# A two-layer hybrid trunk on one core: the recurrence's inverse as two factors with a squared matrix, and values products of causal attention for two blocks of queries at a time

## Chip, cores and metric

The kernel runs on one core of a Trainium2 chip. A core has TensorE (PE: matmuls and transposes, with its weight loads in a row of their own, PEld), VectorE (DVE), ScalarE (ACT), GpSimd (POOL) and SyncE (SP, which here only issues the loads and stores, "DMA"). The metric is the time of one execution of the whole program on the device in microseconds (us); the result is a median of several runs.

## The reference

The input is x, 512 positions of width 1024, with 256 memory tokens. Each of two layers projects x onto about 10,000 columns, feeds four branches of width 512 from them, multiplies each by a gate, projects it back, adds them up with sigmoid gates, projects once more and normalizes with the residual. The change touches two branches and the gate of one.

```python
for l in range(DEPTH):
    h = x @ w_in[l]
    ...
    y_rwkv = _rwkv7_branch(rw_p, rw_g, ...)     # recurrence, 8 heads of 64
    y_mla = _mla_branch(q_lat, kv_lat, ...)     # causal attention, 8 heads
    y_conv = ...; y_mem = ...
    proj = einsum('bsnc,ncd->bsnd', stack(branches), w_o_branch[l])
    merged = sum(sigmoid(merge + b_gate[l]) * proj, axis=2)
    x = layer_norm(ALPHA * x + merged @ w_out[l])

# recurrence, per head, state 64x64, one step per position t
sa = einsum('bhvk,bhk->bhv', state, a_t)
state = state * w_t + sa[..., None] * b_t + v_t[..., None] * k_t
y_t = einsum('bhvk,bhk->bhv', state, r_t)       # then group norm, bonus, * silu(gate)

# causal attention, 128 queries at a time
s = einsum('bqhd,bkhd->bhqk', q_blk, k) * scale     # masked to key <= query
o = einsum('bhqk,bkhd->bqhd', softmax(s), v)
```

## The kernel before

**Wide matmuls.** Activations lie channel by channel: 128 channels on the partitions, 512 positions in the free dimension. The projections are matmuls of a 128x128 weight block with a 128x512 activation. For precision weights and activations are split into a high and a low part (w48h, w48l; xh, xl), and each product is made of three matmuls, of type fp32r. There are thousands of these, and they depend on little else, so they serve as filler under everything that has a chain. In the trace their targets are called ps_m (merge gates), po (output of a branch), ps_rg (gate of the recurrence's branch) and so on; mt, tm and merged are the gated sums on VectorE; w214 is the 214th weight block.

**Order of the work.** The program is written out by `Plan` (lines 59 to 190), which keeps an approximate clock for each engine while it is built. There is a stream of wide items and a list of small tasks (Python generators). At each point the plan takes a task whose operands are due and otherwise the next item. A task that yields "small" runs small matmuls; it is held up to 3000 ns (GATHER) so that several tasks' small matmuls stand together. `shape` charges a switch of the array's cut. The costs used are in `MM` (lines 264 to 284), `Engine.call` and `dma`. The order of each engine is then fixed: on the chip an engine takes its instructions in exactly this order and waits where an operand is not there. So in the trace nearly all matmuls have line 282 (`MM`), transposes 287, operations of VectorE, ScalarE and GpSimd 231 and loads 294, and they are told apart by names.

**The recurrence** (`rwkv_unit`) handles 64 positions at once in closed form. A unit is one pair of heads with four such chunks, half of the sequence: 4 pairs times 2 halves times 2 layers are 16 units. A unit needs the inverse of a 64x64 matrix with unit diagonal, made from a strictly triangular M, for two heads and four chunks: eight 64x64 problems. All small matmuls use a quarter of the array (64x64 cut), four at a time ("quads"), in fp32; each leaves two rows in the trace.

- The four 16x16 diagonal blocks are inverted by substitution on GpSimd (lines 792 to 831): M's blocks go through memory (scr) to W, then 14 steps, and the inverse and its transpose come back through memory as zc and tc (16 columns per block). Z and T are the same, spread by the mask bm to block-diagonal 64x64 tiles.
- Two levels then double the block, from 16 to 32 and to 64 (lines 887 to 952), each with two matmul stages and an evacuation between. x0: M times half the columns of T (width 32), with NQ times vt (nv, an operand of a later step) in the same stage; ScalarE copies to X, VectorE copies nv to RA. dt, dz: Z times X and X times Z (width 32); VectorE copies them with the masks lvm into T and Z (`copy_predicated`). x1: M times T, copied to X. dy: X times Z, copied by mask into Z. X is zeroed once per layer and only partly overwritten.
- va is then Z times RA, followed by the gb/hh/y0 products, the four-step chain of states (w0 to w3) and yb, the output. VectorE takes statistics of yb (gs, gm), GpSimd a power (gr), VectorE scales yb, TensorE transposes it (ty), and yr is the branch's output.

**Causal attention** (`pair`, `mla_block`, lines 1400 to 1478): per layer four pairs of heads; per pair four blocks of 128 queries for each of two heads. A block computes scores (ms), softmax (mP), its transposes (mt) and their copy on ScalarE (mPT, at most four buffers of 512 columns). When both heads' block i is there, their products with the values follow as one "small" group: 2(i+1) matmuls of a 128x64 cut into mo. So there are groups of 2, 4, 6 and 8 matmuls (twice as many rows), four per pair.

**Gates.** `gate_items` multiplies a branch's output by silu of its projection. rg (number 0, the recurrence's) may start when the whole recurrence is done (`"rwkv" in L`), so it comes at the layer's end, ahead of the last merge.

Of the kernel before, what the change touches and what calls it, by code (L numbers as in the profile page):

```python
# [46 lines left out]
for _n, _c in _PARTS:  # L47
# [5 lines left out]
    ("ident", 128), ("bones2", 2), ("reset", 256), ("rn", 8), ("mstr", 64),  # L53
    ("minc", 64), ("bm", 4), ("id2", 64),
# [207 lines left out]
def trunk_kernel(ctx: ExitStack, tc: tile.TileContext, A, out, dbg=None):  # L262
# [4 lines left out]
    def MM(o, lhsT, rhs, start, stop, four=False):  # L267
# [5 lines left out]
        if m <= 64 and n < 16:  # L273
            c = 20.0
        elif rhs.dtype != F32 or n < 16:
            c = max(0.4167 * n + 13.0, 109.0) * (2 if rhs.dtype == F32 else 1)
        elif m <= 64:
            c = (0.42 if four else 0.83) * n + 1.0
        else:
            c = 1.667 * n + 5.0  # L280
# [57 lines left out]
    ident, bones2, reset = cc("ident"), cc("bones2"), cc("reset")  # L338
    lvm = cp.tile([128, 3, 64], U8, tag="lvm", name="lvm")
# [17 lines left out]
    def constants():  # L357
        DMA(cst, A["cst"])
        t = u("lvm32", 192, I32)
        DMA(t, A["lvm"])  # L360
# [5 lines left out]
        def run():  # L366
            V.tensor_copy(lvm, t.rearrange("p (a b) -> p a b", a=3))
# [227 lines left out]
    def layer_items(l):  # L595
# [62 lines left out]
        def begin_rwkv(get):  # L658
# [7 lines left out]
            L["X"] = L["rp"].tile([128, 4, 64], F32, tag="X", name="X" + t_)  # L666
            G.memset(L["X"], 0.0)
# [46 lines left out]
        def rwkv_unit(j, hf, r, k, v):  # L714
# [72 lines left out]
            for b in range(1, 4):  # L787
                V.scalar_tensor_tensor(out=Mc, in0=M[:, :, 16 * b:16 * b + 16], scalar=bm[:, b:b + 1], in1=Mc, op0=ALU.mult, op1=ALU.add)
            d1, d2 = scr[un % 2]
# [4 lines left out]
            def substitution():  # L794
# [27 lines left out]
                zc, tc_ = rk2("zc", "zc" + t, [4, 16], 2), rk2("tc", "tc" + t, [4, 16], 2)  # L822
# [5 lines left out]
                zt.extend((zc, tc_))  # L828
# [57 lines left out]

            yield lambda: L["subs"] > un
            zc, tc_ = zt
            plan.due(zc, tc_)
            yield  # L890
            Z, T, X = rk2("Z", "Z" + t, [4, 64]), rk2("T", "T" + t, [4, 64]), L["X"]
            for dst, src in ((T, tc_), (Z[:, 0:2], chunks(zc)[:, 0]), (Z[:, 2:4], chunks(zc)[:, 1])):
# [5 lines left out]
            def second(x, i):  # L898

                return x.rearrange("p e (d i k) -> p e d i k", d=2, i=2)[:, :, :, i, :]  # L900

            def pairs(x, i):
                return x.rearrange("p e w -> p (e w)").rearrange("p (e q i k) -> p e q i k", e=2, q=4, i=2)[:, :, :, i, :]

            def four(x):
# [1074 lines left out]
```

## Time and profile before

| | |
|---|---|
| median of 3 runs | 1552.19 us (1551.77 to 1552.38) |
| the profiled execution, own time | 1550.24 us |
| its span in the trace | 1548.5 us |
| instructions | 30167 |
| bytes moved by DMA | 153.21 MB, mean 99 GB/s |
| mean granted TensorE clock | 0.997 |

How to read it: a line of the timeline has the start in us from the span's start, the duration, engine, line, operation, out<-in, rows by columns of the array used, and the shape. "x16" are sixteen rows in sequence, and "[2.12 <-DVE yb L231]" is idle time ahead of the instruction with what ended it. Matmuls overlap in the pipeline: a duration is longer than the distance to the next start, and it is the starts that count. A line of the groups has the busy time in all and the mean in ns, then the idle time ahead of them. A line of the windows has the stretch, its length, the busy time of each engine with the number of instructions, the granted clock, the share of the DMA engines and GB/s.

### The profile page before, as it was taken

The page shows a single profiled execution, that of the slowest core. Times are in us where ns is not written, and L with a number is a line of the kernel's source. Part 1 is how long each engine was busy: PE and PEld are TensorE (multiplying, and loading weights), DVE is VectorE, ACT ScalarE, POOL GpSimd, SP SyncE. Part 2 cuts the span into 40 slices and gives each one's busy share as a digit, 9 for nine tenths or more (in the row PEclk, how much of TensorE's full clock was granted, in tenths as well). Part 3 has the DMA queues.
Part 4 walks back from the last instruction along what each step waited for, and adds up shares of the span by engine and source line. Part 5 has one row for each costly group of instructions (what it writes and reads, how often), then busy time and mean ns, then how long its engine had stood idle before and what let it go on. Part 6 is the DMA issues. An engine that isn't in the chain of part 4 may idle for free.

```text
span 1548.5 us, 30167 instructions
## 1 busy us (share of the span) xinstructions
PE 1519.8 (98%) x11912; PEld 1248.3 (81%) x11912; DVE 1111.7 (72%) x2488; ACT 642.3 (41%) x1387; POOL 237.5 (15%) x588
## 2 busy tenths in 40 slices
PE   8999999999999999999999999999999999999997
PEld 8878788877777777888998877788777777777886
DVE  6789888888567765545655888888876777645747
ACT  5546654433244332343364464534334343323332
POOL 0000000433214330000000000002533323300002
PEclk9999999999999999999999999999999999999999
DMA  6452422322222232423343234223222222225231
GB/s 211 129 158 65 116 82 82 90 88 61 86 85 63 72 92 83 149 96 126 123 140 119 83 102 118 75 95 96 65 85 75 75 78 75 75 96 177 95 113 65
DMA packets 81358, 153.21 MB, mean 99 GB/s; under 512 B 33216, under 2 KB 39360, under 8 KB 81216
## 3 DMA queue, kind: packets, MB, share of 16 engines
q1 hardware_dynamic: 81216, 151.28, 31.2%
q8 instruction: 93, 1.52, 0.4%
q14 instruction: 49, 0.40, 0.1%
HBM read 133.95 MB, written 5.77 MB: 90 GB/s over the span
## 4 chain that ended last, share of the span: by engine, by line
PE 86%; DVE 5%; DMA 3%; ACT 2%; POOL 1%; issue 1%; SPq 0%; ACTq 0%; DVEq 0%; POOLq 0%
PE ps_m L282 22%; PE po L282 11%; PE ps_mg L282 3%; PE ps_k L282 3%; PE ps_r L282 3%; PE ps_rg L282 3%; PE ps_v L282 3%; PE ps_xg L282 3%; PE ps_cg L282 3%; PE ps_xq L282 3%; PE ms L282 2%; PE ps_glu L282 2%; PE pz L282 2%; PE pl L282 2%; PE ps_val L282 2%; PE mo L282 1%
## 5 line engine op out<-in xcount | busy, mean ns | idle before, releaser
L231 DVE SCALAR_TENSOR_TENSOR cacc<-hpad,prm,cacc 128x512 f32<-128x512 f32 x240 | 180.2, 753 | 3.5
L231 ACT ACTIVATE tm<-ps_m,prm 128x512 f32<-128x512 f32 x64 | 44.1, 689 | 170.4 <-PE ps_m L282 166.2
L231 POOL TENSOR_TENSOR ZT<-ZT,tmpW 32x14 f32<-32x14 f32 (+6 forms) x224 | 85.7, 383 | 17.6
L231 POOL TENSOR_TENSOR tmpW<-ZT,W 32x14 f32<-32x14 f32 (+6 forms) x224 | 84.1, 375 | 16.1
L231 DVE SCALAR_TENSOR_TENSOR mt<-tm,po 128x512 f32<-128x512 f32 x48 | 33.0, 687 | 74.4 <-PE po L282 69.3
L231 POOL MEMSET X<- 128x256 f32 x2 | 0.6, 314 | 325.1 <-DVE mo L231 165.4
L231 POOL TENSOR_SCALAR gr<-gm 128x4 f32<-128x4 f32 x16 | 4.3, 267 | 288.2 <-DVE gm L231 288.2
L231 POOL TENSOR_SCALAR lrs<-lmv 128x1 f32<-128x1 f32 x8 | 1.7, 207 | 284.4 <-DVE lmv L231 284.4
L231 POOL TENSOR_SCALAR ZT<-W 32x256 f32<-32x256 f32 x16 | 7.8, 490 | 231.4 <-DMA W<-scr 84.2
L231 ACT ACTIVATE mP<-ms,nmm 128x128 f32<-128x128 f32 (+3 forms) x64 | 33.6, 527 | 19.4 <-DVE nmm L231 17.3
L231 DVE SCALAR_TENSOR_TENSOR S<-w,dpad,H 128x64 f32<-128x64 f32 x48 | 13.5, 281 | 31.1 <-PE w L282 30.9
L231 DVE TENSOR_TENSOR merged<-merged,mt 128x512 f32<-128x512 f32 x48 | 33.3, 693 | 1.7
L231 DVE TENSOR_REDUCE nmm<-ms 128x1 f32<-128x128 f32 (+3 forms) x64 | 30.3, 485 | 0.8 <-PE ms L282 0.3
L231 ACT COPY mPT<-mt 128x128 f32<-128x128 f32 (+3 forms) x64 | 26.1, 428 | 10.4 <-PE mt L287 9.9
L287 PE MATMUL mt<-cst,mP 128*128 128x128 f32 x160 | 27.1, 278 | 1.2 <-DVE smm L231 0.8
L231 DVE TENSOR_SCALAR mP<-mP,smm 128x128 f32<-128x128 f32 (+3 forms) x64 | 24.8, 387 | 2.3
L231 ACT CAST rbh<-w 128x256 fp32r<-128x256 f32 x16 | 6.5, 406 | 44.5 <-DVE w L231 44.5
L231 ACT COPY X<-x 128x128 f32<-128x128 f32 x32 | 8.4, 263 | 38.9 <-PE x L282 38.7
L287 PEld LDWEIGHTS mt<-cst,mP 128*128 128x128 f32 x160 | 18.7, 140 | 7.1 <-issue 1.2
L282 PE MATMUL mo<-mPT,v 128*64 128x128 f32 x320 | 24.3, 282 | 0.0
L231 ACT ACTIVATE xP<-xs,nmx 128x256 f32<-128x256 f32 x32 | 15.2, 476 | 20.1 <-DVE nmx L231 19.8
L231 ACT ACTIVATE z<-z,lnb,lrs 128x256 f32<-128x256 f32 (+1 forms) x16 | 9.6, 648 | 32.2 <-DVE lnb L231 32.2
(3512 smaller groups left out, 5469.0 us busy)
## 6 DMA issues: line engine op xcount, KB each, us to landing
w<-in_w_ch_dram SPq DMA_DIRECT2D x146, 512.0 KB, 3.8
w<-in_w_o_dram SPq DMA_DIRECT2D x32, 512.0 KB, 3.8
w<-in_w_out_dram SPq DMA_DIRECT2D x16, 512.0 KB, 3.7
w<-in_w_lat_dram SPq DMA_DIRECT2D x16, 336.0 KB, 3.0
w<-in_w_mk_dram SPq DMA_DIRECT2D x8, 512.0 KB, 3.9
w<-in_w_mv_dram SPq DMA_DIRECT2D x8, 512.0 KB, 3.6
w<-in_w_qk_dram SPq DMA_DIRECT2D x8, 320.0 KB, 2.8
x<-in_xT_dram SPq DMA_DIRECT2D x8, 256.0 KB, 6.1
```

What stands on the lines that cost most here:

```text
L231: return self.plan.keep(f(*a, **k))
L282: plan.keep(nc.tensor.matmul(o, lhsT, rhs, start=start, stop=stop))
L287: plan.keep(nc.tensor.transpose(o, i, ident))
```

## The change

**Inverse.** With D the block-diagonal inverse (Z, and its transpose T) and M multiplied by a new mask moff that keeps only the parts between different 16-blocks, P = M·T is block-triangular with four block rows, so its fourth power is zero, and the inverse is a product of two factors, one from P and one from its square. Three stages: x0 makes P, its transpose PT and nv (three sets of eight matmuls of width 64); x1 makes P times Z and the square of P (two sets); x2 makes the product of PP (square plus unit matrix) and QQ (P times Z, plus Q) (one set). Q is a third copy of the blocks, spread by bm, loaded with one more DMA (zq). lvm, its load and cast, and X are gone. P, RA and the result Zi are copied by ScalarE, PT by VectorE; VectorE adds QQ and PP. The mask `reset` of a scan is made by GpSimd in bf16 and is no longer in the constants.

**Attention.** A values group waits for two blocks of both heads: blocks 0 and 1, then 2 and 3, which are 6 and 14 matmuls, two groups per pair. Blocks 0 and 1 of one head share one mPT buffer; there are still four buffers.

**Gates.** rg's piece i may start when 2i+2 units are done, or when the last branch but this one is fully added.

**The plan's costs** of small matmuls are other numbers, which moves instructions throughout.

```diff
-        if m <= 64 and n < 16:
-            c = 20.0
+        if max(k, m) <= 64:
+            c = max(0.42 * n + 1.0, 29.0) if four else max(0.83 * n + 12.0, 59.0)
...
+            V.tensor_tensor(out=M, in0=M, in1=cc("moff")..., op=ALU.mult)
...
+                DMA(zq, dz.rearrange("(e p t) -> p e t", e=4, t=16))
...
-            Z, T, X = rk2("Z", "Z" + t, [4, 64]), rk2("T", "T" + t, [4, 64]), L["X"]
+            T, Q, Zd = (rk2(n, n + t, [4, 64]) for n in "TQZ")
...
             for cp, c2, h in quads:
-                MM(xv[HALF[h], c2, cp].rearrange("p (d k) -> p d k", d=2), M[HALF[c2], 2 * h + cp], second(T, 0)[HALF[c2], 2 * h + cp], start=True, stop=True, four=True)
+                MM(pv[HALF[h], c2, cp], M[HALF[c2], 2 * h + cp], T[HALF[c2], 2 * h + cp], start=True, stop=True, four=True)
+            for cp, c2, h in quads:
+                MM(tv[HALF[h], c2, cp], T[HALF[c2], 2 * h + cp], M[HALF[c2], 2 * h + cp], start=True, stop=True, four=True)
...
-            S.copy(pairs(X, 0), four(xv))
-            V.tensor_copy(by2(RA)[:, :, :, 0:64], nv)
+            P, PT = rk2("T", "P" + t, [4, 64]), rk2("PT", "PT" + t, [4, 64])
+            S.copy(by2(P), pv)
+            V.tensor_copy(by2(PT), tv)
+            S.copy(by2(RA)[:, :, :, 0:64], nv)
...
-                MM(dT[HALF[c2], h, cp]..., Z[HALF[h], e], second(X, 0)[HALF[h], e], start=True, stop=True, four=True)
+                MM(qv[HALF[c2], h, cp], P[HALF[h], e], Zd[HALF[h], e], start=True, stop=True, four=True)
...
-                MM(dz[HALF[c2], h, cp]..., X[HALF[h], e], second(Z, 1)[HALF[h], e], start=True, stop=True)
+                MM(pv[HALF[c2], h, cp], PT[HALF[h], e], P[HALF[h], e], start=True, stop=True, four=True)
...
-            V.copy_predicated(pairs(T, 0), lv(0), four(dT))
-            V.copy_predicated(pairs(Z, 1), lv(1), four(dz))
+            PP, QQ = rk2("T", "PP" + t, [4, 64]), rk2("PT", "QQ" + t, [4, 64])
+            V.tensor_tensor(out=by2(QQ), in0=qv, in1=by2(Q), op=ALU.add)
+            V.tensor_tensor(out=by2(PP), in0=pv, in1=cc("id2")..., op=ALU.add)
...
-                MM(xv[HALF[h], c2, cp], M[HALF[c2], 2 * h + cp], T[HALF[c2], 2 * h + cp, 0:32], start=True, stop=True, four=True)
-            S.copy(by2(X)[:, :, :, 0:32], xv)
...
-                MM(dz[HALF[h], e], X[HALF[h], e], Z[HALF[h], e, 32:64], start=True, stop=True)
-            V.copy_predicated(Z[:, :, 32:64], lvm[:, 2, 0:32]..., dz)
+                MM(zv[HALF[h], c2, cp], PP[HALF[c2], 2 * h + cp], QQ[HALF[c2], 2 * h + cp], start=True, stop=True, four=True)
+            Z = rk2("Z", "Zi" + t, [4, 64])
+            S.copy(by2(Z), zv)
...
-            left = [4]
+            left = [2]
...
+            if i > 1:
+                PT = m("mPT" + q, 512, "mPT", 4)
+            else:
+                if h not in two:
+                    two[h] = m("mPT" + q, 512, "mPT", 4)
+                PT = two[h][:, 128 * i:]
+            PT = two[h, i] = PT[:, 0:n]
             S.copy(PT, ps)
...
-            if both[1 - h] is None:
+            done.append(q)
+            if len(done) < 4:
                 return
             yield "small"
...
-        gate_items(0, CH_RG, "rg", lambda i: "rwkv" in L, L["yr"], Y[0], bias)
+        gate_items(0, CH_RG, "rg", lambda i: L["units"] >= 2 * i + 2, L["yr"], Y[0], bias)
```

Three places of the program show how this moves instructions. The first is TensorE at the first inverse stage (x0) of the last unit (1_3_1: layer 1, pair 3, second half). Before:

```order
L282 MATMUL po23_1_16485<-ycg1h_1_15820,w206l1_16215 128x512
L282 MATMUL w3_1_3_0_16479<-S2_1_3_0_16470,Gs_1_3_0_16354 64x64 x2
L282 MATMUL x0_1_3_1_16475<-T_1_3_1_16454,M_1_3_1_15971 64x32 x8
L282 MATMUL x0_1_3_1_16475<-vt_1_3_1_16423,NQ_1_3_1_16438 64x64 x8
L282 MATMUL po23_1_16485<-ycg2l_1_15927,w206h1_16214 128x512
```

After:

```order
L282 MATMUL po21_1_16577<-ycg1h_1_15913,w206l1_16398 128x512
L282 MATMUL x0_1_3_1_16576<-T_1_3_1_16547,M_1_3_1_16090 64x64 x8
L282 MATMUL x0_1_3_1_16576<-M_1_3_1_16090,T_1_3_1_16547 64x64 x8
L282 MATMUL x0_1_3_1_16576<-vt_1_3_1_16445,NQ_1_3_1_16456 64x64 x8
L282 MATMUL po21_1_16577<-ycg2l_1_16026,w206h1_16397 128x512
```

The set of width 32 has become two of width 64, and the w3 step of the unit before, which shared the cut here, stands elsewhere. The second place is VectorE at the end of layer 1's recurrence, from the sum of the last yb to yr3, which needs its transpose ty (mt and merged belong to merge gates, w213 to w215 are weights of the rg gates). Before:

```order
L231 TENSOR_TENSOR yb_1_3_1_16870<-yb_1_3_1_16849,Y0_1_3_1_16760 128x2x2x64
L231 BN_STATS gs_1_3_1_16875<-yb_1_3_1_16870 128x6 x4
L231 BN_AGGR gm_1_3_1_16876<-gs_1_3_1_16875 128x2 x4
L231 SCALAR_TENSOR_TENSOR mt27_1_16906<-tm27_1_16891,po27_1_16893 128x512
L231 TENSOR_TENSOR merged7_1_13401<-merged7_1_13401,mt27_1_16906 128x512
L231 TENSOR_SCALAR yb_1_3_1_16870<-yb_1_3_1_16870,gm_1_3_1_16876,gr_1_3_1_16885 128x64 x4
L231 SCALAR_TENSOR_TENSOR yr3_1_16635<-ty_1_3_1_16913,prm1_8674,bon_1_3_1_16111 128x128 x2
```

After:

```order
L231 TENSOR_TENSOR yb_1_3_1_16942<-yb_1_3_1_16910,Y0_1_3_1_16813 128x2x2x64
L231 TENSOR_TENSOR w214l1_16954<-w214_16925,w214h1_16953 128x512
L231 BN_STATS gs_1_3_1_16957<-yb_1_3_1_16942 128x6 x4
L231 BN_AGGR gm_1_3_1_16958<-gs_1_3_1_16957 128x2 x4
L231 TENSOR_SCALAR yb_1_3_1_16942<-yb_1_3_1_16942,gm_1_3_1_16958,gr_1_3_1_16967 128x64 x4
L231 SCALAR_TENSOR_TENSOR mt25_1_17002<-tm25_1_16982,po25_1_16984 128x512
L231 TENSOR_TENSOR merged5_1_12893<-merged5_1_12893,mt25_1_17002 128x512
L231 SCALAR_TENSOR_TENSOR yr3_1_16634<-ty_1_3_1_16995,prm1_8727,bon_1_3_1_16279 128x128 x2
```

The scaling of yb no longer stands behind a merge's mt and sum, but ahead of one. The third place is TensorE in the second values group of layer 1's third pair (mo2) and ScalarE beside it. TensorE after, where the group of before (blocks 2) was alone:

```order
L287 MATMUL mt301_1_11745<-cst_81,mP301_1_11698 128x128 x2
L282 MATMUL mo2_1_11416<-mPT202_1_11622,v0_1_10368 64x128
L282 MATMUL mo2_1_11416<-mPT212_1_11630,v0_1_10368 64x128
L282 MATMUL mo2_1_11416<-mPT202_1_11622,v1_1_10369 64x128
L282 MATMUL mo2_1_11416<-mPT212_1_11630,v1_1_10369 64x128
L282 MATMUL mo2_1_11416<-mPT202_1_11622,v2_1_10370 64x128
L282 MATMUL mo2_1_11416<-mPT212_1_11630,v2_1_10370 64x128
```

ScalarE after:

```order
L231 ACTIVATE mP310_1_11710,smm310_1_11712<-ms310_1_11679,nmm310_1_11711 128x128
L231 CAST yxg3h_1_11736<-xy3_1_11251 128x512
L231 COPY mPT213_1_11739<-mt213_1_11721 128x512
L231 COPY mPT300_1_11680<-mt301_1_11745 128x256
```

Behind the rows shown TensorE continues with mPT203 and mPT213 in the same group. mPT213 lies in the buffer that mPT202 had, so its copy follows the last product with mPT202. The copy of mt301 goes into the tile of mPT300: two blocks share it.

More of the change, by code (lines that the diff above doesn't have):

```diff
@@ L277, in MM @@
         elif m <= 64:
[L278 removed]
+            c = 0.83 * n + 3.0
         else:
@@ L953, in rwkv_unit @@
+            S.copy(by2(Z), zv)
+            pg.free()
             yield
@@ L1510, in count @@
                     picked[n] += 1
-                ch_item(base + i, f"{name}{i}", after, lambda i=i: ready(i), count)
+                ch_item(base + i, f"{name}{i}", after, lambda i=i: ready(i) or n == 0 and added[2] == 8, count)
         def fin(d, h, lo):
@@ L1921, in layout @@
     a["pos"] = positions[0].reshape(4, 128).T
-    a["cst"], a["lvm"], a["once"] = _constants()
+    a["cst"], a["once"] = _constants()
     cuts = np.cumsum([1664, 512, 384, 256, 32, 512, 1024, 512, 512, 512, 4096])
```

85 lines of the change are left out of this document (31 added, 54 removed).

## The prediction

> **What bounds the kernel now.** I read the page first (busy shares, then the chain that ended last), then TensorE's waits, then the timeline around the edited code. The page's busy shares and the chain by engine:
>
> ```profile
> PE 1519.8 (98%) x11912; PEld 1248.3 (81%) x11912; DVE 1111.7 (72%) x2488; ACT 642.3 (41%) x1387; POOL 237.5 (15%) x588
> PE 86%; DVE 5%; DMA 3%; ACT 2%; POOL 1%; issue 1%; SPq 0%; ACTq 0%; DVEq 0%; POOLq 0%
> ```
>
> TensorE is busy for 98% of a 1548.5 us span and holds 86% of the chain. So the time is TensorE's work plus a few holes; a vector or scalar operation counts only where TensorE runs dry. Its waits (total, times, longest) in the places that the change touches:
>
> ```profile
> PE ty L287 <- DVE yb L231: 2.1, 1, 2.1
> ...
> PE bo L282 <- DVE Z L231: 0.4, 1, 0.4
> PE dy L282 <- DVE bon L231: 0.3, 1, 0.3
> ```
>
> Over 16 units the whole recurrence makes TensorE wait 2.1 us once and under half a microsecond twice. Shortening its chain of evacuations is therefore worth nothing by itself. What can be won is array time, and "98% busy" does not show it: switching the array's cut between wide 128x512 matmuls and small 64-row ones counts as busy. I price that as the time from the start of the last wide matmul before a small group to the start of the eighth wide one after it (by then the pipeline is level), less eight wide pitches. The x0 stage of one unit, on TensorE's timeline:
>
> ```profile
> 300.57 0.39 PE L282 MATMUL ps_mg<-xh,w48l 128*128 128x512 f32 x1
> 300.89 0.43 PE L282 MATMUL x<-T,M 64*64 64x32 f32 x16
> 301.14 0.44 PE L282 MATMUL x<-vt,NQ 64*64 64x64 f32 x16
> ...
> 303.23 0.39 PE L282 MATMUL ps_m<-xh,w49h 128*128 128x512 f32 x1
> ```
>
> Each fp32 matmul leaves two rows, so x16 is a set of eight. Sets of width 32 and of width 64 follow alike (0.43 and 0.44), so widening P from 32 to 64 columns should be nearly free; sets and stages count.
>
> **The recurrence, stage by stage.** The other stages of before: dt with dz, then x1, then dy (from 314.03 on):
>
> ```profile
> 1327.23 0.39 PE L282 MATMUL ps_m<-xh,w203l 128*128 128x512 f32 x1
> ...
> 1330.11 0.39 PE L282 MATMUL ps_m<-xh,w203h 128*128 128x512 f32 x1
> ```
> ```profile
> 310.03 0.39 PE L282 MATMUL po<-yxg1h,w50l 128*128 128x512 f32 x1
> ...
> 312.44 0.39 PE L282 MATMUL ps_m<-xh,w51h 128*128 128x512 f32 x1
> ...
> 314.03 0.39 PE L282 MATMUL ps_m<-xh,w51l 128*128 128x512 f32 x1
> ...
> 316.65 0.39 PE L282 MATMUL ps_m<-xh,w51h 128*128 128x512 f32 x1
> ```
>
> From 312.44 to 314.03 seven wide matmuls start: 1.59/7 = 0.227 us each, eight make 1.816. Prices: x0 2.66 - 1.816 = 0.84; dt/dz 2.88 - 1.816 = 1.06; x1 2.41 - 1.816 = 0.59; dy 2.62 - 1.816 = 0.80. A unit pays 3.31 us in four stages.
>
> After has three: x0 with three sets of width 64, x1 with two, x2 with one. Before never runs exactly these, so I take like groups: x0 with nv and a yb set (three sets, from 1138.61), x0 with nv (two, above), a yb set alone (from 337.35); and, for shared cuts, yb with dt and dz (from 412.60).
>
> ```profile
> 1138.61 0.40 PE L282 MATMUL po<-yxg3h,w177l 128*128 128x512 f32 x1
> ...
> 1141.51 0.39 PE L282 MATMUL ps_mg<-xh,w179h 128*128 128x512 f32 x1
> ```
> ```profile
> 337.35 0.39 PE L282 MATMUL ps_m<-xh,w54l 128*128 128x512 f32 x1
> ...
> 339.79 0.39 PE L282 MATMUL ps_m<-xh,w54h 128*128 128x512 f32 x1
> ```
> ```profile
> 412.60 0.39 PE L282 MATMUL po<-ymg1h,w63l 128*128 128x512 f32 x1
> ...
> 415.71 0.39 PE L282 MATMUL ps_r<-xh,w64h 128*128 128x512 f32 x1
> ```
>
> x0 2.90 - 1.816 = 1.08, x1 0.84, x2 2.44 - 1.816 = 0.62: 2.55 us. The saving is 3.31 - 2.55 = 0.76, times 16 units 12.1 us. Bounds: x0 from 0.84 (two sets) to 1.29 (yb, dt and dz: 3.11 - 1.816), x1 from 0.62 to 1.06, x2 from 0.59 to 0.80, which gives 2.05 to 3.15 and a saving of 20.1 to 2.5. I keep the middle, because those groups have the right number of sets; for the range I take some 4 us to each side, since all three ends would have to fall together.
>
> Something is given back. In TensorE's order the 64x64-cut stretches go from 141 to 130, not to 125: five stages that stood beside another small group now stand alone. Sharing is worth 0.62 + 1.06 - 1.29 = 0.39, so five cost 2.0. Recurrence: 12.1 - 2.0 = **10.1 us less**.
>
> The vector work, from the groups by line:
>
> ```profile
> L231 DVE COPY RA<-x 128x256 f32<-128x256 f32 x16 | 6.7, 420 | 3.0 <-ACT X L231 2.9
> L231 DVE TENSOR_TENSOR Gs<-gb,cst 128x256 f32<-128x256 f32 x16 | 6.6, 415 | 0.0
> L231 DVE COPY_PREDICATED Z<-lvm,dz 128x128 f32<-128x128 uint8 x16 | 4.7, 294 | 0.4
> ```
>
> VectorE adds the PT copy (0.42), the moff product, the Q mask and the QQ and PP adds (0.415 each), and loses the RA copy (0.42, now on ScalarE) and three predicated copies (0.294): 0.78 us a unit, 12.5 in all. I cost it at nothing: VectorE is 72% busy, and between two stages of a unit TensorE's order holds 13 or more wide matmuls (2.9 us), as before. Without that cover it would cost the 12.5. The further 32 KB load per unit (zq) goes to SP's queue behind tc; SPq has 0% of the chain. Nothing too for the lvm load and X memsets that go and for the reset mask, built once by GpSimd. Layer 1's recurrence starts 72 wide matmuls later; all that is filler in another order, free as long as the recurrence's end stays covered (below).
>
> **The values products.** The cost of a 128x64-cut group, a sixteen-row one and the start of a twelve-row one:
>
> ```profile
> 940.19 0.39 PE L282 MATMUL xo<-xPTh,vml 128*128 128x512 f32 x1
> 940.50 1.09 PE L282 MATMUL mo<-mPT,v 128*64 128x128 f32 x16
> 941.53 0.50 PE L282 MATMUL ps_glu<-xl,w149h 128*128 128x512 f32 x1
> ...
> 943.25 0.39 PE L282 MATMUL ps_glu<-xh,w149h 128*128 128x512 f32 x1
> ```
> ```profile
> 200.01 0.88 PE L282 MATMUL mo<-mPT,v 128*64 128x128 f32 x12
> 200.82 1.09 PE L287 MATMUL mt<-cst,mP 128*128 128x128 f32 x8
> ```
>
> The sixteen rows cost 3.06 - 1.816 = 1.24. They take 1.03 to the next start, twelve take 0.81: 0.055 a row, 0.88 for sixteen, and 0.36 is fixed. The rows stay the same; the stretches go from 31 to 16: 15 x 0.36 = **5.4 us less**.
>
> Against it stands one new wait. In layer 1's third pair (mo2), mPT213 now takes the buffer of mPT202, which products of the same group still read. TensorE stands in the group for one copy and its hand-overs.
>
> ```profile
> L231 ACT COPY mPT<-mt 128x512 f32<-128x512 f32 x16 | 9.1, 587 | 3.3 <-PE mt L287 3.2
> ```
>
> 0.59 of copy and, an estimate, 0.4 for the way to ScalarE and back: **1.0 us more**, from 0 (if wide matmuls are ready behind it, which TensorE's fixed order excludes) up to the 7 of the second rival.
>
> **The gates and the end of layer 1.** There before has its one big hole, TensorE first and then VectorE:
>
> ```profile
> 1400.82 0.39 PE L282 MATMUL po<-ycg3h,w212l 128*128 128x512 f32 x1
> 1403.33 0.68 PE L287 MATMUL ty<-cst,yb 128*128 128x128 f32 x2 [2.12 <-DVE yb L231]
> ...
> 1405.32 0.76 PE L282 MATMUL ps_rg<-xh,w214l 128*128 128x512 f32 x1 [0.83 <-DVE w214l L231]
> ...
> 1408.84 0.39 PE L282 MATMUL ps_rg<-xh,w214h 128*128 128x512 f32 x1
> ```
> ```profile
> 1401.32 0.69 DVE L231 SCALAR_TENSOR_TENSOR mt<-tm,po 128x512 f32<-128x512 f32 x1 [3.00 <-ACT w215h L231]
> ...
> 1402.65 0.98 DVE L231 TENSOR_SCALAR yb<-yb,gm,gr 128x64 f32<-128x64 f32 x4
> ```
>
> From 1400.82 to 1408.84 are 8.02 us with eleven wide matmuls (2.50) and two transposes (0.2, an estimate from the eight in 1.09 above): 5.3 us lost. 2.12 is the wait for yb, whose scaling stands behind mt27 and merged7 on VectorE, which wait for the last product; 0.83 is a weight that came late; 1.7 is half clock: from 1405.32 eight wide ones take 3.52 and not 1.82.
>
> ```profile
> 1400.00:1410.00 10.00, 6.99 (x24) 4.89 (x23) 5.29 (x12) 1.28 (x3) 0.00 (x0) 0.83 0.25 84
> ```
>
> The granted clock of this window is 0.83 (the column ahead of the DMA share). After has rg0 and rg1 inside the recurrence, 33 wide matmuls (7.5 us) between the last yb and ty, and the scaling straight behind its statistics on VectorE. In before the mt27 pair and its idle time take 4.3 us (from 1401.32 - 3.00 = 1398.32 to 1402.65; the row names w215h, but po27's last product, the row at 1400.82, ended only 0.1 before). Without these ty's input is ready in time, so the hole closes: **5.3 us less**.
>
> The Trainium skill ("TensorE: Matmul & The Clock Gate", What's actually happening) puts the half clock after at least one idle window of about 3.4 us. Here the trace differs: two gaps of 2.12 and 0.83 us, with work between, were followed by it.
>
> **Sum.** -10.1 - 5.4 - 5.3 + 1.0 = -19.8 on the profiled execution (1550.24): 1530.4. The median of the runs is 1552.19, 1.95 above it: **1532.4 us**.
>
> **The rivals.**
>
> 1. The hole stays. rg2 and rg3 still come last, and their weights may again not be there. Against it: 33 wide matmuls of other work, and two gates fewer. Without the 5.3: 1537.7.
> 2. The shared PT buffers stall every pair. Four buffers now hold two blocks of both heads until a group has run; if each of the eight pairs paid the 1.0 once, 7 more: 1539.4. For it: ScalarE runs in order, so a copy that waits holds back the casts behind it. Against it: only one pair has the copy and its reader in one group.
> 3. The half clock stays though the waits go, because it hangs on some other idle stretch: 1.7 come back, 1534.1. By the Trainium skill's rule it would not be these gaps that caused it. For the forecast speaks the order: idle first, half clock right behind.
> 4. The change does nothing for the time: switches overlap with weight loads, and wide matmuls take back what the small ones free. Against it: the prices are end to end. 1552.
> 5. Slower: evacuations become the bound. There are 48 stage hand-overs (16 x 3) and VectorE has 12.5 us more. A hand-over needs 0.83 there (QQ and PP), against 2.9 of cover; TensorE waits once VectorE is about 2 us behind, three of its wide operations. From 19.8/48 = 0.41 us per hand-over the gain is gone; at 0.6 it is 28.8 - 19.8 = 9 slower, 1561. Against it: bo and dy above, 0.4 and 0.3 us in all.
>
> The Trainium skill ("TensorEngine Tiling (Array Packing)", PSUM Bottleneck) warns of just that: "After 4× TensorE speedup, PSUM copy may become bottleneck".
>
> **How the numbers follow.** Chances: forecast 0.72, rivals 0.10, 0.08, 0.05, 0.02 and 0.03. The range starts 4 below the forecast (the small groups' bounds), 1528, and reaches over rivals 1 to 3 to 1541; outside are rivals 4 and 5 and the forecast's tails, some 0.15. A measurement of this kernel tells 0.2%, 3.1 us, from no change; every case but the last two is faster by more: 0.95, 0.02, 0.03.
>
> **What would show it.** Right: TensorE's busy time down by some 15 us, no wait of ty on yb, granted clock 1.0 at the end of layer 1, sixteen mo stretches with one wait for mPT of about 1 us. Wrong: waits of x1, x2 or va on VectorE or ScalarE (rival 5), of mo on mPT in several pairs (2), of ty or ps_rg (1); or a three-set x0 group that costs more than 1.3 us end to end.

## The result and the profile after

The changed kernel took 1541.34 us (median of 4 runs, 1539.05 to 1542.45) beside 1551.98 for the kernel before: a ratio of 0.9933, 95% interval 0.9916 to 0.995. It is faster by 10.6 us; 19.8 were forecast. Measured again later (run e5 below) it took 1537.42 beside 1551.39, 0.9911 (0.9895 to 0.9927).

The page of the changed kernel, busy shares and the chain by engine, shows little of it: TensorE's busy time is down by 9.4 us, where the prediction looked for some 15, and VectorE's share of the chain is 8% where it was 5%.

```profile
PE 1510.4 (98%) x11912; PEld 1244.7 (81%) x11912; DVE 1124.6 (73%) x2503; ACT 648.5 (42%) x1403; POOL 238.7 (15%) x588
PE 84%; DVE 8%; DMA 3%; ACT 2%; issue 1%; POOL 1%; SPq 0%; ACTq 0%; DVEq 0%; POOLq 0%
```

The array prices can be measured with the prediction's yardstick (last wide start ahead of the group to the eighth behind it, less 1.816). TensorE's timeline of the changed kernel, x0, then x1, then x2:

```profile
305.04 0.39 PE L282 MATMUL ps_m<-xh,w49l 128*128 128x512 f32 x1
305.36 0.46 PE L282 MATMUL x<-T,M 64*64 64x64 f32 x16
305.64 0.41 PE L282 MATMUL x<-M,T 64*64 64x64 f32 x16
305.87 0.41 PE L282 MATMUL x<-vt,NQ 64*64 64x64 f32 x16
...
307.94 0.39 PE L282 MATMUL ps_m<-xh,w49h 128*128 128x512 f32 x1
```
```profile
375.25 0.39 PE L282 MATMUL ps_m<-xh,w58l 128*128 128x512 f32 x1
...
377.92 0.39 PE L282 MATMUL ps_m<-xh,w58h 128*128 128x512 f32 x1
```
```profile
313.98 0.39 PE L282 MATMUL po<-yxg1h,w50l 128*128 128x512 f32 x1
314.30 0.46 PE L282 MATMUL x<-QQ,PP 64*64 64x64 f32 x16
...
316.41 0.39 PE L282 MATMUL ps_m<-xh,w51h 128*128 128x512 f32 x1
```

x0 is 2.90 - 1.816 = 1.08, x1 2.67 - 1.816 = 0.85, x2 2.43 - 1.816 = 0.61: 2.54 us a unit, forecast 2.55. The other units in which these stages stand alone give the same within 0.02. A values group of 28 rows:

```profile
208.07 0.39 PE L282 MATMUL ps_xq<-xh,w33l 128*128 128x512 f32 x1
208.39 1.75 PE L282 MATMUL mo<-mPT,v 128*64 128x128 f32 x28
...
211.79 0.39 PE L282 MATMUL ps_xq<-xh,w33h 128*128 128x512 f32 x1
```

3.72 - 1.816 = 1.90; 28 x 0.055 + 0.36 is 1.90. So the 15.5 us of array time went as forecast. The hole at the end of layer 1 went too: ty has no idle time ahead of it (before: 2.12).

```profile
1393.62 0.38 PE L287 MATMUL ty<-cst,yb 128*128 128x128 f32 x2
```

That is 15.5 + 5.3 = 20.8 us, and the profiled execution fell by 1550.24 - 1542.45 = 7.8. Some 13 us came in elsewhere. TensorE's waits in the changed kernel (what waited, for which operation; total, times, longest) show a part:

```profile
PE bo L282 <- DVE rbl L231: 1.8, 2, 1.0
...
PE mt L287 <- ACT mPT L231: 1.1, 1, 1.1
PE w L282 <- DVE S L231: 1.1, 2, 0.9
PE mt L287 <- DVE mP L231: 0.9, 3, 0.5
...
PE mo L282 <- ACT mPT L231: 0.5, 1, 0.5
```

Before, bo waited 0.4, mt on mP 0.2, and mt on mPT, w and mo did not wait. Adding up TensorE's idle times over 0.05 us (without the start's) gives 12.0 us before and 13.9 after, although 3.0 of the 12.0 have gone: about 5 us of new waits. Each also makes the pipeline fill again: the longest wait of w is 0.91, but from the matmul ahead of it (started at 333.82) to w's first start it is 1.12 longer than usual. Over a dozen waits that would be about 2 us, an estimate. The rest is the clock. The windows, of 3.41 us and one of 6.81, are chosen so that the half-clock stretches fill the second and the fourth:

```profile
100.92:104.33 3.41, 1.35 (x7) 0.81 (x6) 0.98 (x3) 2.04 (x4) 0.00 (x0) 1.00 0.80 238
104.34:107.75 3.41, 3.41 (x9) 2.67 (x10) 2.25 (x4) 0.06 (x1) 0.00 (x0) 0.50 0.63 142
906.47:909.88 3.41, 1.84 (x8) 1.24 (x9) 3.23 (x13) 2.99 (x12) 0.00 (x0) 1.00 0.61 244
909.89:916.70 6.81, 6.81 (x25) 5.42 (x25) 3.50 (x8) 2.98 (x8) 0.00 (x0) 0.50 0.01 2
```

10.2 us at a granted clock of 0.50; the matmuls that start there take 4.9 us more than like pairs elsewhere. And the half clock with which the kernel starts lasted until 12.0 us, before until 9.2: another 1.2 (its first matmuls, pl, start 0.28 apart, later 0.15). 5 of waits, 2 of refilling (the estimate), 4.9 and 1.2 of half clock are the 13.

### The profile page after: what moved, and what is told of

Its sections match the earlier page's. It is cut to its first block, busy times and chain, and to the rows that moved or that the text cites. A ratio compares the mean times of both kernels' runs of the same rounds, so it can differ in the third digit from the quotient of the medians.

```text
span 1540.7 us, 30211 instructions
## 1 busy us (share of the span) xinstructions
PE 1510.4 (98%) x11912; PEld 1244.7 (81%) x11912; DVE 1124.6 (73%) x2503; ACT 648.5 (42%) x1403; POOL 238.7 (15%) x588
## 3 DMA queue, kind: packets, MB, share of 16 engines
q8 instruction: 94, 1.54, 0.4%
## 4 chain that ended last, share of the span: by engine, by line
PE 84%; DVE 8%; DMA 3%; ACT 2%; issue 1%; POOL 1%; SPq 0%; ACTq 0%; DVEq 0%; POOLq 0%
PE ps_m L282 21%; PE po L282 11%; PE ps_cg L282 3%; PE ps_rg L282 3%; PE ps_v L282 3%; PE ps_val L282 3%; PE ps_xg L282 3%; PE ps_k L282 3%; PE ps_r L282 3%; PE ps_glu L282 2%; PE ps_xq L282 2%; PE ps_mg L282 2%; DMA w<-in_w_ch_dram 2%; PE pz L282 2%; PE pl L282 2%; PE ms L282 2%
## 5 line engine op out<-in xcount | busy, mean ns | idle before, releaser
L231 ACT ACTIVATE mP<-ms,nmm 128x512 f32<-128x512 f32 (+3 forms) x64 | 33.8, 530 | 17.6 <-DVE nmm L231 16.3
L231 DVE TENSOR_REDUCE nmm<-ms 128x1 f32<-128x512 f32 (+3 forms) x64 | 30.2, 485 | 1.7 <-PE ms L282 1.6
L231 DVE TENSOR_SCALAR mP<-mP,smm 128x512 f32<-128x512 f32 (+3 forms) x64 | 24.8, 387 | 2.3
L231 ACT ACTIVATE xP<-xs,nmx 128x256 f32<-128x256 f32 x32 | 15.2, 475 | 19.5 <-DVE nmx L231 19.4
L282 PE MATMUL ms<-kTl,qT 96*128 96x512 f32 (+3 forms) x64 | 23.0, 359 | 0.0
L282 PE MATMUL ms<-kTh,qT 96*128 96x512 f32 (+3 forms) x64 | 21.1, 330 | 0.0
L282 PE MATMUL ms<-kTh,qTl 96*128 96x512 f32 (+3 forms) x64 | 21.1, 330 | 0.0
```

Source lines behind the costliest of these rows:

```text
L231: return self.plan.keep(f(*a, **k))
L282: plan.keep(nc.tensor.matmul(o, lhsT, rhs, start=start, stop=stop))
```

## The experiments

The theories: A, the array prices hold and what came back are new waits and half-clock windows in the new order; and rivals to it, the wide stages costing more than their stand-ins (B), the shared mPT buffers (C), and others named in the texts. Times are medians; before's own median beside a run was 1550.8 to 1552.1, so the ratios compare.

**Each part alone.** The hunks of the diff were put into the kernel before one part at a time: e1 the inverse with its masks and loads, e2 `mla_block` and `pair`, e3 the two lines of rg, e4 the plan's costs.

```diff
# e3
-                ch_item(base + i, f"{name}{i}", after, lambda i=i: ready(i), count)
+                ch_item(base + i, f"{name}{i}", after, lambda i=i: ready(i) or n == 0 and added[2] == 8, count)
-        gate_items(0, CH_RG, "rg", lambda i: "rwkv" in L, L["yr"], Y[0], bias)
+        gate_items(0, CH_RG, "rg", lambda i: L["units"] >= 2 * i + 2, L["yr"], Y[0], bias)
# e4
-        if m <= 64 and n < 16:
-            c = 20.0
+        if max(k, m) <= 64:
+            c = max(0.42 * n + 1.0, 29.0) if four else max(0.83 * n + 12.0, 59.0)
...
-            c = (0.42 if four else 0.83) * n + 1.0
+            c = 0.83 * n + 3.0
```

> The kernel before with the new inverse alone (old values groups, old gates, old plan costs). Theory A (the array prices of the prediction hold, and what was lost in the full change is new waits and half-clock windows that the new order made elsewhere): 12.1 us less from three stages instead of four; the order has 133 stretches of 64x64 cut where 141 - 16 = 125 would share fully, so eight shared cuts fewer give back 3.1; about 9 us less end to end, TensorE's total outside idle time and half clock 9 less, and the recurrence adds single waits of 0.5 to 1 us on VectorE. Rival B (the three wide stages cost more array time than their stand-ins): end to end 2 to 5 us less with no new waits that would explain it.

Measured 1538.41, 0.9925 (0.9911 to 0.9939), 12.6 less. In the trace the hole at the end is closed (36 wide matmuls between the last yb and ty), w waits 0.7 and bo 0.7 in all (before 0 and 0.4), and there is no half clock but at the start and the end. Theory A had 9 us less and did not see that this order would close the hole; the 9 us of array price and 4 to 5 of the hole account for the time, and rival B falls.

> The kernel before with the two-block values groups alone. Theory A: 31 to 16 stretches of 128x64 cut, 15 x 0.36 = 5.4 us less, and two 64x64 stretches fewer (0.8): about 6 less, less what transposes (mt) wait for mPT in the pairs. Rival C (the shared PT buffers themselves make the pairs wait): several waits of mt or mo on mPT, 0.5 to 1.1 us each, and less than 3 us gained.

Measured 1551.56, 1.0002 (0.9992 to 1.0012): nothing. Its waits:

```profile
PE ty L287 <- DVE yb L231: 4.5, 1, 4.5
...
PE ps_xq L282 <- DVE xql L231: 1.5, 2, 1.0
...
PE mt L287 <- ACT mPT L231: 1.0, 1, 1.0
```

The array price came: with half-clock time counted half, TensorE's busy time is 5.3 us below that of before. But the order here has no wide matmul at all between the last yb and ty, and ty waits 4.5 instead of 2.1, with 6.8 us at half clock behind it (3.4 before); in layer 0's attention 2.2 us of idle time are new. Together they eat the groups' gain. Neither theory had the end in it at this size.

> The kernel before with only the earlier rg gates. Theory A: the hole at the end of layer 1 (2.1 + 0.8 us idle, 1.4 to 1.7 us half clock) closes, about 5 us less, and no other place moves much. Rival D: the hole goes, but the half clock is a matter of where a window of 3.4 us falls, so that a half-clock stretch comes up at another hole (101 us or 906 us): 3 us less only.

Measured 1546.73, 0.9975 (0.9965 to 0.9985), 4.3 less. The hole is gone, and one half-clock stretch came at 104 us. Between A and D, nearer to A.

> The kernel before with only the plan's new costs for small matmuls: the same instructions in a slightly other order. Theory A: no array price changes (140 and 141 stretches), so the difference, up to 3 us either way, is the size of what order alone does through waits. Rival E (the costs are what made the new waits of the changed kernel): slower by 3 us or more, with waits at 184 us and in the recurrence as in the changed kernel.

Measured 1552.6, 1.0006 (0.9994 to 1.0018). Rival E's 3 us did not come, and mt on mPT does not wait at 184 us; but part of its sign did: w waits 1.26 in the recurrence, at the place where it waits in the changed kernel. So a new order alone is enough for that wait (S, which w needs, stands here on VectorE behind sums of the convolution and a part of w55; no load is late). This order closes the end hole as well (33 wide matmuls) and opens waits of ct and zw; its profiled execution, at full clock but for its start and end, was at 1546.95, its median 5.7 above that.

**Parts taken out or put together.** e5 is the changed kernel once more, e7 it without the values groups, e11 without the gates, e12 without the costs, e8 the inverse with the gates alone (the same hunks as above). e6 adds an mPT buffer:

```diff
-U_SLOTS = 32
+U_SLOTS = 31
...
-                PT = m("mPT" + q, 512, "mPT", 4)
+                PT = m("mPT" + q, 512, "mPT", 5)
...
-                    two[h] = m("mPT" + q, 512, "mPT", 4)
+                    two[h] = m("mPT" + q, 512, "mPT", 5)
```

> The changed kernel again, for more runs of it on one chip beside the next three. Theory A: median 1541 (+-2), with runs 1.7 or 3.4 us apart as the half-clock windows fall; the same waits as in its first profile (mt on mPT 1.1, bo 1.0, w 0.9, mo on mPT 0.5). Rival: the first profile's waits were chance, and its median is near 1532 to 1536.

Measured 1537.42 (1536.28 to 1538.16), below theory A's 1539 to 1543 and above its rival's 1532 to 1536. The waits are theory A's: those of the first profile, within 0.3 us but for mt in layer 1 (0.85 where it was 0.17; 0.70 before). The half-clock stretches in the middle are not there, and its profiled span is 1535.7 against 1540.7. So the waits belong to the order, the half clock to the execution. Without those stretches TensorE's busy time is 15.2 us below that of before, as the prediction had it:

```profile
PE 1504.6 (98%) x11912; PEld 1240.8 (81%) x11912; DVE 1124.2 (73%) x2503; ACT 648.7 (42%) x1403; POOL 237.5 (15%) x588
```

> The changed kernel with a fifth mPT buffer and one of the 32 general 512-column buffers less; the order of every engine stays the same. Theory A (the pairs wait because the stage is bound by VectorE, ScalarE and late weights, not by the buffers): only the 0.46 us wait of mo at 987 us goes, median within 1 us of the changed kernel. Rival C (shared buffers make the pairs wait): the waits of mt and mo on mPT go, 1.1 + 0.5 + about 0.9 behind them, 2 to 4 us less.

Measured 1537.39, 0.9912 (0.9898 to 0.9925): no gain. mo's 0.46 wait is gone, and in this run mt's on mPT was 0.2. But in e10, which has the five buffers too, mt waits 0.9 again: that wait does not hang on the buffers, and rival C falls for it. Two later waits of mt do in part: 0.23 and 0.53 to 0.58 at 192 to 198 us with four buffers, 0.3 in all in each kernel with five (e6, e10, e17). The edit has a price too: with one general buffer less xo waits 0.34, which it does nowhere else, and pq at 103 us 2.8 to 3.0 where the changed kernel has 2.1 to 2.2, while xt at 905 us waits 0.4 to 0.8 for 1.2.

> The changed kernel with the old values groups (31 stretches of 128x64 cut instead of 16, 64x64 stretches 130 as in the changed kernel). Theory A: the stretches' 5.4 us are paid again, but the waits in layer 0's attention (0.5 + 1.1 + 0.2 + 0.5 idle) go: 0 to 2 us slower than the changed kernel, at most equal. Rival (the values groups do give their 5.4 in the full change): 4 to 6 slower, 1546.

Measured 1539.57, 0.9929 (0.9915 to 0.9944), on the chip of e5 and 2.15 above it. The intervals overlap; by the medians the values groups give about 2 us in the full change, not 5.4. In the two profiles TensorE works 4.4 us longer without the groups (half-clock time counted half) and is idle for 3.4 less than in e5. The wait of ps_xq at 158 us is 0.06 here and 0.50 to 0.53 in every kernel with the new groups; mt's two waits at 192 to 198 us (0.23 and 0.53 to 0.58 in the changed kernel) are not there either.

> The kernel before with the new inverse and the earlier gates, without the new values groups and the new plan costs (134 stretches of 64x64 cut). Theory A: the inverse alone had -8.8 of array price and closed the end hole by its order, so the gates add nothing to it: 1537 to 1540, as the inverse alone. Rival (parts add up: -12.6 and -4.3): 1534.

Measured 1540.41, 0.9938 (0.9921 to 0.9956): just above theory A's 1537 to 1540, far from its rival's 1534. The gates add nothing to the inverse; the hole was closed already.

> The changed kernel with the old gates (rg only when the whole recurrence is done). 27 wide matmuls stand between the last yb and ty (18 in the kernel before, 33 in the changed one, none with the values groups alone, where ty waited 4.5 us). Theory A (the hole goes by the number of matmuls between, whichever part of the change puts them there): no wait of ty, within 2 us of the changed kernel. Rival (the gates are what closes it): the 5 us hole is back, 1542.

Measured 1538.76, 0.9909 (0.9893 to 0.9924). ty does not wait, as theory A has it:

```profile
1382.71 0.46 PE L282 MATMUL yb<-S,B 64*64 64x64 f32 x16
1389.36 0.38 PE L287 MATMUL ty<-cst,yb 128*128 128x128 f32 x2
```

6.65 us lie between, filled with 27 wide matmuls. The gates are not needed to close the hole in the full change.

> The changed kernel with the plan's old costs (134 stretches of 64x64 cut instead of 130). Theory A: four shared cuts fewer cost 1.6, and other waits than those of the changed kernel come up: 0 to 3 us slower. Rival E (the new costs made the new waits): the waits in the recurrence and at 182 us go, 2 us or more faster.

Measured 1536.66, 0.9903 (0.9888 to 0.9918): no difference that can be told from the changed kernel. w at 331 waits 0.47 and bo at 488 0.76, as in the changed kernel; bo at 1186 does not wait and mt on mPT only 0.31, but ps_r at 1231 (0.67) and bo at 1328 (0.36) are new. Rival E's 2 us did not come.

**Who holds up TensorE.** e9 writes the RA copy ahead of the PT copy; e10 does that with five buffers.

```diff
             S.copy(by2(P), pv)
-            V.tensor_copy(by2(PT), tv)
             S.copy(by2(RA)[:, :, :, 0:64], nv)
+            V.tensor_copy(by2(PT), tv)
```

The ground for it, from the groups of the changed kernel (ScalarE's RA copy) and of e9 (RA, then VectorE's PT):

```profile
L231 ACT COPY RA<-x 128x256 f32<-128x256 f32 x16 | 6.0, 372 | 32.6 <-DVE PT L231 32.6
```
```profile
L231 ACT COPY RA<-x 128x256 f32<-128x256 f32 x16 | 6.1, 379 | 0.0
...
L231 DVE COPY PT<-x 128x256 f32<-128x256 f32 x16 | 6.7, 419 | 5.5 <-ACT RA L231 5.4
```

> The changed kernel with the RA copy written ahead of the PT copy; every engine's order stays the same, only who waits for whom on x0's tile changes: ScalarE's RA no longer waits for VectorE's PT (32.6 us of ScalarE's idle time in 16 units), PT waits for RA. Theory A (that wait holds back the casts behind RA and so w, rbl and bo): the waits of bo at 489 and 1186 us (0.75 and 1.09) go or halve, 1 to 2 us less than the changed kernel. Rival (VectorE's own backlog is the cause): bo's waits stay, no difference.

Measured 1537.77, 0.9905 (0.9891 to 0.9919); its profiled execution was the shortest of all those profiled, 1533.82. ScalarE's 32.6 us ahead of RA are gone; bo waits 0.34 where it waited 1.09 (1186 us), w 0.24 for 0.69, but bo at 488 still 0.93. The mechanism is shown for the first of them, which waits 0.98 to 1.18 in the changed kernel, e5, e6 and e15 (e16 and e17 below, with delays of their own, have 0.37 without the edit and 1.20 with it); the median cannot be told from the changed kernel's.

> Both: RA ahead of PT, and the fifth mPT buffer of the earlier run. Theory A: the waits of mt at 182 us and mo at 983 us (1.2 and 0.46) and of bo go together, 2 to 4 us less than the changed kernel, about 1534 where that has 1537.4. Rival: waits move on to the next late operand, no difference.

Measured 1535.11, 0.9892 (0.9878 to 0.9906). The waits of bo at 1186, of w at 332 and of mo are gone; bo at 489 still waits 0.77, mt on mPT 0.9, mt in layer 1 1.0. It is the fastest median of the study, but its interval overlaps that of the changed kernel.

e13 and e14 shorten an operation of VectorE in the attention, in the kernel before and in the values groups alone; e15 three of the inverse's in the changed kernel. They leave that work out; the plan is charged the old cost, so the orders stay.

```diff
# e13, e14
-            V.tensor_scalar(out=P, in0=P, scalar1=sm, scalar2=None, op0=ALU.mult)
+            plan.op("DVE", 70 + 0.85 * n, _names(P), _names(sm))
+            plan.keep(nc.vector.tensor_scalar(out=P[:, 0:1], in0=P[:, 0:1], scalar1=sm, scalar2=None, op0=ALU.mult))
# e15 (and PP, QQ = P, PT; moff and QQ in the same way)
-            V.tensor_tensor(out=by2(PP), in0=pv, in1=cc("id2")..., op=ALU.add)
+            plan.keep(nc.vector.tensor_tensor(out=PP[:, 0:2, 0:1], in0=pv[:, 0, :, 0:1], in1=cc("id2")[:, 0:2].unsqueeze(2), op=ALU.add))
```

> The kernel before, with the scaling of the softmax (mP times smm, 64 operations of 0.39 us on VectorE) done on one column only: leaves that work out, every engine's order stays. It is the base for the next run. Theory A: TensorE was 99.8% busy in layer 0's attention, so nothing or 1 us is gained (1550 to 1551 where before has 1551).

> The two-block values groups alone, with the same scaling on one column only: leaves that work out, the order is that of the run with the values groups alone. Theory F (in the attention VectorE with its chain to ScalarE and back is as late as TensorE, and takes back what the groups save): with VectorE relieved the waits of mt and ps_xq in layer 0 go and the groups' 6 us appear against the run before this one, except 2 to 2.4 us for the longer wait of ty at the end: 3.5 to 5 us less. Rival G (buffers, late weights): the waits stay and it is within 1.5 us of the run before this one.

Measured 1550.47, 0.9991 (0.9982 to 1.0), and 1551.69, 0.9996 (0.9987 to 1.0004). Theory F falls by the waits: with VectorE relieved ps_xq waits its 0.50 and mt 0.52 (196 us); only mt's 0.23 is gone, and its wait on mPT is 0.2 (0.2 to 1.2 over the runs anyway). The times alone say less, since e14 has the longer wait of ty with 6.8 us at half clock behind it, and e13 no half clock there.

> The changed kernel with the moff product and the QQ and PP adds of the inverse done on one or two columns only (leaves that work out; 1.25 us a unit less on VectorE, more than the 0.78 that the change added), orders unchanged. Theory H (the recurrence's new waits, bo 0.75 and 1.09, w 0.7 to 0.9, come from VectorE's added work): these waits go and 2.5 to 3.5 us are gained with the drains behind them, 1534. Rival (late weights and ScalarE's order behind a copy): bo and w wait as before, less than 1 us gained.

Measured 1539.13, 0.9907 (0.989 to 0.9925): nothing gained, theory H falls. The waits:

```profile
PE w L282 <- DVE S L231: 2.1, 2, 1.9
...
PE bo L282 <- DVE rbl L231: 1.5, 2, 1.2
```

Only bo at 492 us is shorter (0.35 for 0.75). Where w waits, the changed kernel's timeline has SyncE issuing weight loads behind a substitution's transfers, ScalarE waiting for such a load, VectorE for ScalarE, and S, which w needs, behind both on VectorE:

```profile
325.13 0.34 SPq L294 DMA_DIRECT2D scr<-ZT  x1
...
329.14 1.93 SPq L294 DMA_DIRECT2D w<-in_w_ch_dram  x2
```
```profile
333.35 1.14 ACT L231 CAST w54h<-w 128x512 fp32r<-128x512 f32 x2 [3.95 <-DMA w<-in_w_ch_dram]
334.00 0.69 DVE L231 TENSOR_TENSOR w54l<-w,w54h 128x512 fp32r<-128x512 f32 x1 [1.23 <-ACT w54h L231]
334.61 0.28 DVE L231 SCALAR_TENSOR_TENSOR S<-w,dpad,H 128x64 f32<-128x64 f32 x1
...
334.95 0.33 PE L282 MATMUL w<-S,Gs 64*64 64x64 f32 x4 [0.91 <-DVE S L231]
```

The same pattern is read, not tested, behind mt's wait on mPT in layer 0: the copies of mt are queued behind the cast of w33, which waits 1.95 us for its load.

```profile
183.05 0.62 ACT L231 CAST w33h<-w 128x512 fp32r<-128x512 f32 x1 [1.95 <-DMA w<-in_w_ch_dram]
183.57 0.47 ACT L231 COPY mPT<-mt 128x384 f32<-128x384 f32 x1
```

**Late loads.** SyncE issues weight loads and the substitution's transfers in one queue. e16 has GpSimd issue the latter in the changed kernel, e18 in the kernel before, e17 together with e10's two edits.

```diff
             def substitution():
...
-                DMA(d1.rearrange("(c p t) -> p c t", c=4, t=16), Mc)
+                DMAG(d1.rearrange("(c p t) -> p c t", c=4, t=16), Mc)   # nc.gpsimd.dma_start; all six alike
```

> The changed kernel with the six loads and stores of each substitution issued by GpSimd, which computes it, and not by SyncE; the orders of TensorE, VectorE and ScalarE stay the same, and weight loads no longer stand in SyncE's queue behind transfers that wait for GpSimd (159 us of SyncE's waiting for ZT). Theory I (late weights: a block's load stands behind those transfers, its cast holds up ScalarE and VectorE, and w or bo waits): the wait of w at 332 us (0.7 to 1.9 in five runs) goes and bo's at 489 shrinks, 1.5 to 3 us less than the changed kernel. Rival (the waits come from the order of ScalarE and VectorE alone): w and bo wait as before, nothing gained.

Measured 1553.75, 1.0021 (1.001 to 1.0031): 16 us slower than the changed kernel. The wait of w at 332 us is gone as theory I has it, but the edit brought costs of its own. GpSimd's groups and TensorE's waits:

```profile
L301 POOL DMA_DIRECT2D zc<-scr x32 | 19.9, 626 | 0.0
...
L301 POOL DMA_DIRECT2D scr<-Mc x16 | 12.7, 794 | 558.0 <-DVE Mc L231 558.0
```
```profile
PE ct L287 <- DVE cn L231: 5.7, 2, 3.5
PE bo L282 <- DVE rbl L231: 3.5, 4, 1.6
```

GpSimd spends 0.54 to 0.79 us on each issue and stands 558 us before the store of Mc. Where ct waits 3.5 us, the power of the convolution's norm (crs), on which ct depends, stands in GpSimd's queue behind the store of ZT, the wait for it and the loads of tc, zq and zc:

```profile
1141.30 0.77 POOL L301 DMA_DIRECT2D tc<-scr  x1 [3.27 <-DMA scr<-ZT]
...
1144.12 0.18 POOL L231 TENSOR_SCALAR crs<-cmv 128x1 f32<-128x1 f32 x1
```

So the run tells only of the one wait, and not of that alone: e10 has no wait of w there either, and it moves no load to another queue.

> The second queue, RA ahead of PT and the fifth mPT buffer together. Theory I: the waits of w, bo and mo in the recurrence and in mo2 go together, about 1533 where the before has 1552 (ratio 0.988). Rival: no better than the last two of these, 0.989 to 0.9905.

Measured 1551.41, 1.0001 (0.999 to 1.0012): the same costs (ct 5.9, bo 5.4).

> The kernel before with its substitution's loads and stores issued by GpSimd. If theory I is about the new order (weights are late only in the changed kernel, whose load of zq and later start of units moved them), nothing changes here: within 1 us of before, since w has no wait there. Rival (a general gain of a second queue): 2 us or more faster here too, and then it explains nothing of the difference.

Measured 1555.88, 1.003 (1.0019 to 1.0041): neither, slower by 4 to 5 here too.

## Why the prediction was wrong

- **Recurrence, 10.1 less: right.** 2.54 us a unit against 2.55, with 130 stretches in the trace too. Widening the sets was nearly free, as their rows had it (a set alone costs 0.61 where the narrow x1 cost 0.59).
- **VectorE's added work at nothing: right, but for one copy.** Taking 1.25 us a unit away from VectorE gained nothing (e15), and neither x1, x2 nor va waits in the changed kernel, although the cover is a little thinner than the "13 or more": 12 wide matmuls in several places, 9 once. The copies' change of engines was costed at nothing as well, and there one wait came in: ScalarE's RA now stands behind VectorE's PT (e9).
- **Values groups, 5.4 less: the price was right, the gain was not.** The group costs what was worked out, but in the full change the groups give about 2 us (e7), alone none (e2, where the end of layer 1 takes back more than the attention does). Layer 0's attention answers with waits of 0.5 (ps_xq) and 0.2 and 0.5 (mt) that only kernels with these groups have. VectorE's scaling explains the 0.2 at most (e14); a fifth buffer takes 0.5 off mt's two, but adds waits elsewhere (e6). What sets that of ps_xq and the rest is open.
- **End hole, 5.3 less: right, but only one of the two reasons given.** The prediction named 33 wide matmuls and a shorter way on VectorE. The way is no shorter: from the start of the last yb matmuls (1385.60) to the end of the scaling it is 7.1 us in the changed kernel, 7.2 before; now parts of weights stand ahead of the statistics. The scaling:

```profile
1391.69 0.98 DVE L231 TENSOR_SCALAR yb<-yb,gm,gr 128x64 f32<-128x64 f32 x4 [1.41 <-POOL gr L231]
```

In e4 VectorE even has the order of before, mt ahead of the scaling and 7.2 us, and 33 wide matmuls close the hole. What decides is how many of them stand between the last yb and ty, against that way: 0 gave a wait of 4.5 us, 18 gave 2.1, 27 (e11, where the way is 4.4) and more none. Nor does it take the gates: it is closed with the inverse alone, with the costs alone, and in the change without the gates. So the parts alone cannot be added up: each counts the same hole.

- **The step that failed is the sum's last term, the new waits at 1.0.** The prediction went through the order, found one new wait (mPT213, 1.0) and took all other hand-overs as covered because "TensorE's order holds 13 or more wide matmuls (2.9 us)" between stages. That one wait was 0.46; the 0.4 that the prediction put on top of the copy, for the way to ScalarE and back, stands in no row. The new waits were 5 us of idle time in the first profile (5.7 in e5) and some 2 of refilling, an estimate. The largest stand not behind the stage copies that were counted, but behind something ahead of them in an engine's queue: a cast that waits for a late load (w, mt on mPT: read from the timeline, and for w e16 fits, but in e4 w waits without a late load), a copy that waits for another engine's copy of the same tile (bo at 1186: e9). For the other waits the cause is open. Rivals 2 and 5 had such waits as one mechanism each; here they are several, and small, and none of the prediction's signs of being wrong looked at them.
- **The clock, which is luck.** The prediction booked the half clock of the end hole as gone with the hole. But half-clock stretches come at other holes too, in some executions, and the first profile lost 4.9 us to them at two holes that the kernel before has as well. Without them (e5) the profiled execution was at 1537.48, 12.8 less than the 1550.24 of before: 20.8 less 8 of waits and refilling. The mean granted clock was 0.995 to 0.997 in the first four runs and 0.996 to 0.998 in e5's four; how much of the 3.9 us between their medians is the clock is open.

## What to carry to other kernels

Array time saved was forecast here to a few hundredths of a microsecond a stage from groups of like sets in the trace; it is worth that much only if nothing else in the program's order moves. Where a planner writes the order anew, take a loss for new waits from the start (here 8 of 20.8 us), and look for it in each engine's queue ahead of the operation, not in the operation's own chain. Parts that each close the same hole alone must not be added.

## What was not expected of the hardware

The half clock comes in windows on a grid of 3.413 us that lies differently in every execution: in the first profile they start at 104.338 and 909.883 us, 236.0 windows apart. A window at half clock follows one in which TensorE was busy for little: 1.35 and 1.84 of 3.41 us above. In e5 the same hole fell across two windows, and the window behind each stayed at full clock:

```profile
99.33:102.74 3.41, 1.65 (x8) 1.03 (x6) 0.84 (x2) 1.44 (x3) 0.00 (x0) 1.00 0.84 251
102.75:106.15 3.40, 2.96 (x13) 2.47 (x14) 2.85 (x5) 1.25 (x4) 0.00 (x0) 1.00 0.71 157
```

Over the twenty profiles every window at full clock with up to 1.4 us busy was followed by one at half clock, none with 2 or more, and between them it went either way (1.48, 1.65 and 1.87 without; 1.54, 1.84 and 1.92 with). So one hole of 2 us costs 2 us in one execution and some 3.5 in another: behind the hole at 104 us the same matmuls took 1.45 us longer in the first profile than in e5. The Trainium skill ("TensorE: Matmul & The Clock Gate", What's actually happening) has the window free-running, 4096 cycles or 3413 ns, which the trace bears out; its rule that the half clock follows an idle window is too strict here, as these windows were up to 56% busy.
